# A bank for the first block's fourth product, two row statistics taken at other ticks, and a reordered end, in a one-core encoder-layer kernel

## The chip, the cores and the metric

The kernel runs on one core of a Trainium2 chip. The metric is the device time of one execution in microseconds (us). The kernel before was run three times: 2029.69, 2029.9 and 2030.85 us, median 2029.9 us.

The names of the profile: PE is the matrix engine (TensorE), PEld its weight loads, DVE is VectorE, ACT is ScalarE, POOL is GpSimd, and SP is the engine whose queue starts most of the transfers (SPq). L718 means line 718 of the kernel before.

## The reference

One encoder layer over 512 tokens of width 2048, in float32:

```python
xn   = rms_norm(x, attn_norm_g)
u_val, u_gate, q, k, v = split(xn @ w_in)
y_conv = conformer_conv(u_val, u_gate, ...)     # GLU, depthwise conv of 31, layer norm, silu
y_na   = neighborhood_attention(q, k, v, rpb)   # 16 heads on an 8 x 64 grid of tokens
mixed  = concat(rms_norm(y_conv, conv_out_g), rms_norm(y_na, na_out_g))
x = x + mixed @ w_out
up = depthwise_conv(rms_norm(x, ffn_norm_g) @ w_up, ffn_dw_w, ffn_dw_b)   # width 3
gate, val = split(up)                                                     # 5632 each
x = x + (silu(gate) * val) @ w_down
out = rms_norm(x, final_norm_g)
```

## The kernel before, in words

**Layout.** Activations stand transposed: 128 channels on the partitions, the 512 tokens along the free dimension, in tiles of 128x512 (`t2`, 79 buffers). Each float32 product is made of three matmuls of rounded operands: weights are split into a high and a low part (`parts`, L113, one pass on ACT at L116 and one on DVE at L117), activations likewise, and `mm3` (L124, matmuls at L127 to L129) adds high x high, high x low and low x high in a PSUM bank.

**Order.** The program is written in plain order, and a planner with a cost table for each instruction decides the order on each engine: among the instructions that its model takes as ready, the one written first goes first. Each engine then runs its queue strictly in that order. `pin` keeps an instruction behind the one that was written before it on its engine, and `issue_after` keeps a block's instructions behind a given one. On PE this is used by `tick` (L134): after each unit of 24 matmuls of a projection, it takes one further step of the generators in `steps` (attention, statistics) and `asteps` (the convolution group), whose matmuls so stand behind that unit. Each `yield` in a generator is one unit of delay.

**PSUM.** There are three banks with the tag `mm` for products, one bank `po`, two banks `tr` and one pair `sc`. A product that asks for a tag waits until a bank of this tag is released by its last reader.

**Statistics.** `rsqrt_steps` (L179) turns a sum of squares per token into a row of factors: eight small matmuls with a column of ones add over the partitions (L190), `root` (L172) takes 1/sqrt with one Newton step, the result is laid on two diagonal tiles `dg` (L197 to L201), and one tick later two matmuls with ones (L207) spread it over all partitions, in bank `po`, from which ACT copies it (L211).

`group_a` (L372) is the convolution group: mean (L379), squares (L384 to L386), two idle ticks, the statistic `rln`, then for each of eight tiles the norm, silu and the split into `mah` and `mal` (L393 to L396), `RA_AFTER` = 2 idle ticks, and the statistic `ra`. `out_half(ma, read_a)` (L561, called at L590) is the product with the upper half of `w_out`: sixteen times 24 matmuls, each into an `mm` bank that `read_a` (L580) releases by a DVE product with `ra` (L585). The attention's `values` (L494) also uses the bank `po`, which ACT releases at L507.

**The gated MLP.** The up-projection is done with a Strassen-like scheme of seven products per block f of 128 hidden channels; the first four blocks go through `up_apart` (L793). For f = 0 the products 0 to 2 are written side by side (`first_three`, L811), because the last input tiles come late: seven of the eight inner steps for each, then the eighth for each. The products 0 to 5 take `mm` banks, product 6 takes `po` (`begin`, L795). ACT copies the products 0 and 1 away (L823), the product 2 is added by DVE (L825), ACT copies the product 3 (L826), and the products 4 to 6 are read by DVE (L827, L830, L831).

**The end.** The last four blocks' down-projection is made in two ways. For the tokens 0 to 383, sixteen products `pd` of 128x384 are added to `x2` by DVE (L946), squared by ACT and summed into `acc3` (L947). For the tokens 384 to 511 the result is made token-major in four banks, g = 0 to 3 (L970 to L984): four transposes of `x2` and twelve matmuls each (L973, L977 to L979), a square with a sum on ACT (L981) and a product with the gain on DVE (L984). The banks 0 and 1 are the two halves of one `sc` tile, the banks 2 and 3 are `tr` banks. Between these matmuls, `spread` (L956) takes the steps of the statistic `rstd3` of the first 384 tokens: the column sums after (g, k) = (0, 1), the spreading matmuls of L207 after (1, 0). Then eight pairs of channel tiles are finished (`finish`, L925) and sent out, 128x384 each: in five pairs DVE multiplies straight from the PSUM bank (L935) and each half goes out by a transfer of its own (L937), in three pairs (1, 4, 7) ACT has multiplied by the gain before (L932) and POOL multiplies (L933) by a copy `rb` of the factors in SBUF that ACT makes at L966, with one transfer for the pair (L939). The last 128 tokens are scaled after the root over all four sums (L986 to L997) and leave in four transfers (L998).

Of the kernel before, what the change touches and what calls it, by code (L numbers as in the profile page):

```python
# [10 lines left out]
F32 = mybir.dt.float32  # L11
F32R = mybir.dt.float32r
AF = mybir.ActivationFunctionType
ALU = mybir.AluOpType
AX = mybir.AxisListType

P = 128
D = 2048
S = 512
# [9 lines left out]
EPS = 1e-6  # L29
# [13 lines left out]
CH = 4  # L43
# [8 lines left out]
ORDER = "aavaav" + "aq" * 4 + "qqqq"  # L52
NORM_AT = 4
NG = GW // 8
RA_AFTER = 2

PCOLS = [("g1", KD), ("dww", NC_ * CK), ("dwb", NC_), ("lng", NC_), ("lnb", NC_), ("cog", NC_),
         ("nag", NC_), ("g2", KD), ("fww", 2 * NF * 3), ("fwb", 2 * NF), ("g3", KD)]
# [9 lines left out]
def layer(ctx: ExitStack, tc: tile.TileContext, xT, xG, w_in, w_v, w_out, w_up, w_down, par, tab, g3, out, last_out):  # L68
    nc = tc.nc
# [6 lines left out]
    psa = ctx.enter_context(tc.tile_pool(name="psa", bufs=1, space=bass.MemoryType.PSUM))  # L76
# [9 lines left out]
    def t2(name, dt=F32):  # L86
        return tp.tile([P, S], dt, tag="t2k", name=name)

    def t4(shape, name):

        return wpool.tile(shape, F32, tag="raw", name=name, bufs=NR)

    pin = tc.keep_in_program_order
# [5 lines left out]
    def pc(name, i):  # L99
        o = POFF[name] + i  # L100
        return prm[:, o:o + 1]
# [4 lines left out]
    ident = consts.tile([P, P], F32, name="ident")  # L106
# [41 lines left out]
    def weights():  # L148
        at = weights.at
        weights.at += 1  # L150
        while len(made) < min(at + 1 + AHEAD, len(plan)):
            made.append(plan[len(made)]())
        return made[at]
# [3 lines left out]
    def split(src, g, name):  # L157

        h, l = t2(name + "h", F32R), t2(name + "l", F32R)
        nc.scalar.activation(h, src, AF.Copy, scale=g)  # L160
        nc.vector.scalar_tensor_tensor(l, src, g, h.bitcast(F32), op0=ALU.mult, op1=ALU.subtract)
        return h, l

    def sum_sq(acc, src, first, to=slice(0, S)):
        if first:
            nc.scalar.activation(acc, src, AF.Square)
        else:
            q = t2("sq")[:, to]
            nc.scalar.activation(q, src, AF.Square)
            nc.vector.tensor_add(acc, acc, q)  # L170

    def root(r, y, v):  # L172
        nc.scalar.activation(r, v, AF.Sqrt)
        nc.vector.reciprocal(r, r)
        nc.vector.scalar_tensor_tensor(y, r, -0.5, r, op0=ALU.mult, op1=ALU.mult)
        nc.vector.tensor_mul(y, y, v)
        nc.vector.scalar_tensor_tensor(y, y, 1.5, r, op0=ALU.add, op1=ALU.mult)
# [56 lines left out]
    ps = psa.tile([P, 2, S], F32, tag="sc", name="idle")  # L234
# [22 lines left out]
    for step in ORDER:  # L257
# [5 lines left out]
        i = next(a_ if step == "a" else q_)  # L263
# [108 lines left out]
    def group_a():  # L372
        acc = t2("acc")
        nc.vector.tensor_add(acc, ys[0], ys[1])
        for i in range(2, NC_):
            nc.vector.tensor_add(acc, acc, ys[i])
        yield
        ps = psa.tile([P, S], F32, tag="po", name="st")
        nc.tensor.matmul(ps, ones, acc, start=True, stop=True)  # L379
        mu = t2("mu")  # L380
        nc.vector.tensor_scalar(mu, ps, 1.0 / CONV, None, op0=ALU.mult)
        acc = t2("acc")
        for i in range(NC_):
            nc.vector.tensor_sub(ys[i], ys[i], mu)  # L384
            sum_sq(acc, ys[i], i == 0)
            if i == NC_ // 2 - 1:  # L386
                yield
        yield
        yield
        r = yield from rsqrt_steps(acc, CONV, "rln")  # L390
        acc = t2("acc")
        for i in range(NC_):
            nc.vector.tensor_mul(ys[i], ys[i], r)  # L393
            nc.scalar.activation(ys[i], ys[i], AF.Silu, scale=pc("lng", i), bias=pc("lnb", i))
            ma.append(split(ys[i], pc("cog", i), "ma"))
            sum_sq(acc, ys[i], i == 0)  # L396
            if i % 2:
                yield
        for _ in range(RA_AFTER):
            yield  # L400
        ra.append((yield from rsqrt_steps(acc, CONV, "ra")))


# [151 lines left out]
    x2 = []  # L555
# [237 lines left out]
    def up_apart(f, between):  # L793

        def begin(c):  # L795
            return weights(), (psa.tile([P, S], F32, tag="po", name="pu") if c == 6 else
                               psm.tile([P, S], F32, tag="mm", name="pu"))[:, :H]

        def part(c, w, ps, ks):
            for k in ks:  # L800
                m = comb[c][k]
                i = mm3(ps, w, k, m[:, :H], m[:, H:], k == 0, k == U - 1)
            return i

        def product(c):
            w, ps = begin(c)
            tick(part(c, w, ps, range(U)))
            between(c)
            return ps

        def first_three():  # L811
            got = [begin(c) for c in range(3)]
            for c in range(3):
                tick(part(c, *got[c], range(U - 1)))
            for c in range(3):
                part(c, *got[c], range(U - 1, U))
            return [ps for _, ps in got]

        vv, v, uu, g = (t2(n).rearrange("p (i t) -> p i t", i=2) for n in ("vv", "vl", "uu", "g"))
        both = lambda x: x.unsqueeze(1).broadcast_to([P, 2, H])  # L820
        early = iter(first_three() if f == 0 else map(product, range(3)))
        for i in range(2):
            nc.scalar.activation(vv[:, i], next(early), AF.Copy)  # L823
        u, u2 = uu[:, 0], uu[:, 1]
        add(v, vv, both(next(early)))  # L825
        nc.scalar.activation(u, product(3), AF.Copy)  # L826
        add(u2, u, product(4))  # L827
        add(v, v, both(u2))
        add(vv[:, 1], vv[:, 1], u2)
        add(g[:, 0], u, product(5))  # L830
        add(g[:, 1], vv[:, 1], product(6))  # L831
        return tuple(t.rearrange("p i t -> p (i t)") for t in (g, v))
# [62 lines left out]
    x2, ws = [], []  # L895
# [27 lines left out]
    fm, tm = slice(0, LT), slice(LT, S)  # L923

    def finish(pair, r, apart=False, split=False):  # L925

        o = t4([P, 2, LT], "fin")
        for i in range(2):
            d = 2 * pair + i
            x, g = x2[d][:, fm], pc("g3", d)  # L930
            if apart:
                nc.scalar.activation(x, x, AF.Copy, scale=g)  # L932
                nc.gpsimd.tensor_mul(o[:, i], x, r)  # L933
            else:
                nc.vector.scalar_tensor_tensor(o[:, i], x, g, r, op0=ALU.mult, op1=ALU.mult)  # L935
            if split:
                nc.sync.dma_start(out[pair][:, i], o[:, i])  # L937
        if not split:
            nc.sync.dma_start(out[pair], o)  # L939

    acc = t2("acc3")
    for d in range(KD):
        ps = psm.tile([P, S], F32, tag="mm", name="pd")[:, fm]
# [7 lines left out]
    stats, rb, xg = rsqrt_steps(acc, D, "rstd3", to=fm, keep=False), [], []  # L951
    sums, v, r, y = (sm.tile([P, CH], F32, tag="rs" + c, name="rs" + c) for c in "lvry")
    v, r, y = (t[:, :1] for t in (v, r, y))
    pairs = list(range(KD // 2))

    def spread(g, k):  # L956
        if (g, k) == (0, 1):
            next(stats)
        elif (g, k) == (1, 0):
            try:  # L960
                next(stats)
            except StopIteration as e:
                rb.append(e.value)
            finish(pairs.pop(0), rb[0], split=True)
            rb.append(t2("rb")[:, fm])
            nc.scalar.activation(rb[1], rb[0], AF.Copy)  # L966
        elif rb and pairs:
            at = pairs.pop(0)
            finish(at, rb[at % 3 == 1], at % 3 == 1, at % 3 != 1)

    for g, ps in enumerate(banks):
        for i in range(CH):
            nc.tensor.matmul(ps[:, i * P:(i + 1) * P], x2[g * CH + i][:, tm], ident, start=i == 0, stop=False,  # L973
                             is_transpose=True)
        for k in range(n):
            (hh, hl), (dh, dl) = hs[k], ws[g * CH + k]
            nc.tensor.matmul(ps, hh[:, tm], dh, start=False, stop=False)  # L977
            nc.tensor.matmul(ps, hl[:, tm], dh, start=False, stop=False)
            nc.tensor.matmul(ps, hh[:, tm], dl, start=False, stop=k == n - 1)  # L979
            spread(g, k)  # L980
        nc.scalar.activation(t2("sq"), ps, AF.Square, accum_out=sums[:, g:g + 1])  # L981
        xg.append(t2("xg"))
        if g < CH - 1:
            nc.vector.tensor_mul(xg[g], ps, gains[g])  # L984
        if g == CH - 2:
            nc.vector.tensor_reduce(v, sums[:, :CH - 1], axis=AX.X, op=ALU.add)  # L986
            nc.vector.tensor_scalar(v, v, 1.0 / D, EPS, op0=ALU.mult, op1=ALU.add)
    assert not pairs
    nc.vector.scalar_tensor_tensor(v, sums[:, CH - 1:], 1.0 / D, v, op0=ALU.mult, op1=ALU.add)
    root(r, y, v)  # L990
    for g in range(CH):
        if g == CH - 1:
            nc.vector.scalar_tensor_tensor(xg[g], banks[g], y, gains[g], op0=ALU.mult, op1=ALU.mult)
# [79 lines left out]
```

## Time and profile before

| | |
|---|---|
| time, median of three runs | 2029.9 us |
| the profiled execution | 2030.16 us, of which the profile's span is 2028.4 us |
| PE busy | 2015.4 us (99% of the span) |
| DVE, ACT, POOL busy | 1675.5, 1050.9, 159.5 us |
| granted PE clock, mean | 0.998 |
| output | 4.19 MB in 17 transfers |

How to read it: an engine's busy time is the sum of the time in which at least one of its instructions ran. In rows of the timeline the columns are the start in us from the start of the span, the duration in us, the engine, the line, the operation, what is written and read, the shapes and the count; in brackets stands the time for which the engine had been idle before, and what ended this. Matmuls overlap: each row of a 128x512 matmul says 0.39 us, but the next one starts 0.227 us later, and this distance of the starts is what a matmul costs.

### The profile page before, as it was taken

The numbers are of one execution on the slowest core, as the hardware profiler recorded it, in microseconds if no ns is written. First come the engines' busy times: TensorE is split into PE (matmuls) and PEld (weight loads), VectorE is DVE, ScalarE is ACT, GpSimd is POOL, SyncE is SP. The second block draws the span as 40 slices with busy tenths as digits, with TensorE's granted clock in tenths as the row PEclk, the third lists the DMA queues.
The fourth block names the chain that finished last, engine by engine and source line by source line (L and its number), as shares of the span: only waits on it lengthen the run. The fifth ranks groups of instructions, "written<-read, shape, count | busy, mean of one in ns | idle before, by whom it ended". The sixth has DMA issues, their size and how long they took to land.

```text
span 2028.4 us, 28313 instructions
## 1 busy us (share of the span) xinstructions
PE 2015.4 (99%) x10672; PEld 1726.5 (85%) x10672; DVE 1675.5 (83%) x2298; ACT 1050.9 (52%) x1674; POOL 159.5 (8%) x188
## 2 busy tenths in 40 slices
PE   9999999999999999999999999999999999999998
PEld 7888888888888998888888888888888888888887
DVE  7986888988577898888888888888888888889875
ACT  7323344466346555555555555555555555555563
POOL 0000000000001001111111111111111111110111
PEclk9999999999999999999999999999999999999999
DMA  7232333336347435566565565565565565564583
GB/s 256 83 104 84 114 94 109 109 124 215 108 120 178 120 114 146 123 147 146 125 146 146 128 142 146 128 142 146 121 149 146 125 146 146 127 144 127 144 206 126
DMA packets 97784, 276.41 MB, mean 136 GB/s; under 512 B 10992, under 2 KB 12784, under 8 KB 97648
## 3 DMA queue, kind: packets, MB, share of 16 engines
q1 hardware_dynamic: 72288, 228.45, 36.3%
q0 software_dynamic: 25216, 46.15, 15.5%
q8 instruction: 84, 1.38, 0.3%
q14 instruction: 52, 0.43, 0.1%
q10 hardware_dynamic: 144, 0.01, 0.0%
HBM read 220.04 MB, written 54.53 MB: 135 GB/s over the span
## 4 chain that ended last, share of the span: by engine, by line
PE 96%; DVE 2%; DMA 1%; ACT 0%; issue 0%; SPq 0%; ACTq 0%; DVEq 0%
PE pu L718 25%; PE pu L724 13%; PE pd L129 8%; PE pd L127 8%; PE pd L128 8%; PE pj L127 5%; PE pj L128 5%; PE pj L129 5%; PE po L127 3%; PE po L128 2%; PE po L129 2%; PE pv L313 1%; PE pv L312 1%; PE pv L314 1%; PE pu L127 1%; PE pu L129 1%
## 5 line engine op out<-in xcount | busy, mean ns | idle before, releaser
L116 ACT ACTIVATE whi<-raw 128x1024 fp32r<-128x1024 f32 x364 | 384.4, 1058 | 503.8 <-PE pj L128 136.6
L117 DVE TENSOR_TENSOR wlo<-raw,whi 128x1024 fp32r<-128x1024 f32 x364 | 444.4, 1221 | 214.0 <-ACT whi L116 205.2
L718 PE MATMUL pu<-xc,whi 128*128 128x512 f32 x2240 | 552.9, 391 | 0.0
L718 PEld LDWEIGHTS pu<-xc,whi 128*128 128x128 f32 x2240 | 413.0, 188 | 79.1
L724 PEld LDWEIGHTS pu<-xc,wlo 128*128 128x128 f32 x2240 | 292.3, 191 | 13.9
L724 PE MATMUL pu<-xc,wlo 128*128 128x256 f32 x2240 | 296.6, 283 | 0.0
L129 PE MATMUL pd<-hh,wlo 128*128 128x512 f32 x640 | 250.1, 391 | 0.0
L127 PE MATMUL pd<-hh,whi 128*128 128x512 f32 x640 | 249.6, 390 | 0.0
L128 PE MATMUL pd<-hl,whi 128*128 128x512 f32 x640 | 249.3, 390 | 0.0
L871 POOL DMA_DIRECT2D x2d<-pdc x160 | 139.4, 873 | 1162.4 <-ACT pdc L870 837.4
L128 PE MATMUL pj<-xl,whi 128*128 128x512 f32 x512 | 200.2, 391 | 0.1
L129 PE MATMUL pj<-xh,wlo 128*128 128x512 f32 x512 | 200.0, 391 | 0.0
L127 PE MATMUL pj<-xh,whi 128*128 128x512 f32 x512 | 198.9, 393 | 0.0
L750 ACT ACTIVATE pl<-pu 128x256 f32<-128x256 f32 x280 | 104.6, 382 | 143.5 <-PE pu L718 136.4
L116 ACT ACTIVATE whi<-ws 128x1024 fp32r<-128x1024 f32 x132 | 139.8, 1059 | 75.2 <-PE pu L718 58.2
L366 DVE SCALAR_TENSOR_TENSOR y<-ch,prm,y 128x500 f32<-128x500 f32 (+14 forms) x240 | 173.3, 740 | 4.3
L117 DVE TENSOR_TENSOR wlo<-ws,whi 128x1024 fp32r<-128x1024 f32 x132 | 161.1, 1220 | 13.9 <-ACT whi L116 13.6
L129 PEld LDWEIGHTS pd<-hh,wlo 128*128 128x128 f32 x640 | 120.1, 188 | 28.5 <-DVE wlo L117 3.3
L128 PEld LDWEIGHTS pd<-hl,whi 128*128 128x128 f32 x640 | 120.2, 188 | 24.9 <-DVE hl L856 0.3
L127 PEld LDWEIGHTS pd<-hh,whi 128*128 128x128 f32 x640 | 120.4, 188 | 22.6
L870 ACT ACTIVATE pdc<-pd 128x512 f32<-128x512 f32 x160 | 93.8, 588 | 79.3 <-PE pd L129 65.9
L127 PEld LDWEIGHTS pj<-xh,whi 128*128 128x128 f32 x512 | 96.3, 188 | 20.7 <-ACT xh L249 0.2
(204 smaller groups left out, 2886.4 us busy)
## 6 DMA issues: line engine op xcount, KB each, us to landing
raw<-in_w_up SPq DMA_DIRECT2D x176, 512.0 KB, 3.7
raw<-in_w_down SPq DMA_DIRECT2D x88, 512.0 KB, 4.0
x2d<-pdc POOLq DMA_DIRECT2D x160, 256.0 KB, 4.8
raw<-in_w_in SPq DMA_DIRECT2D x60, 512.0 KB, 3.8
raw<-in_w_out SPq DMA_DIRECT2D x32, 512.0 KB, 3.8
raw<-in_w_v SPq DMA_DIRECT2D x16, 512.0 KB, 4.1
tab<-in_tab SPq DMA_DIRECT2D x32, 256.0 KB, 5.0
x<-in_xG SPq DMA_DIRECT2D x16, 256.0 KB, 5.4
```

The lines of the kernel that those rows point to most:

```text
L116: i = nc.scalar.activation(hi[:, :n], raw[:, :n], AF.Copy)
L117: j = nc.vector.tensor_sub(lo[:, :n], raw[:, :n], hi[:, :n].bitcast(F32))
L127: nc.tensor.matmul(ps, hi[:, a], mh, start=start, stop=False)
L128: nc.tensor.matmul(ps, hi[:, a], ml, start=False, stop=False)
L129: return nc.tensor.matmul(ps, lo[:, a], mh, start=False, stop=stop)
L312: nc.tensor.matmul(ps, xh, wh[:, f], start=kk == 0, stop=False)
L366: nc.vector.scalar_tensor_tensor(y[:, a:b], h[:, a + j - PAD:b + j - PAD], prm[:, o + j:o + j + 1], y[:, a:b], op0=ALU.mult, op1=ALU.add)
L718: i = nc.tensor.matmul(ps, w[0][:, k * P:(k + 1) * P], comb[c][k], start=k == 0, stop=stop and k == ks[-1])
L724: i = nc.tensor.matmul(ps[:, H:], w[1][:, k * P:(k + 1) * P], comb[c][k][:, :H], start=False, stop=stop and k == U - 1)
L750: nc.scalar.activation(to, ps, AF.Copy)
L870: nc.scalar.activation(t, ps, AF.Copy)
L871: nc.gpsimd.dma_start(xd[d], t, accum_op=ALU.add)
```

## The change

- In `group_a` there are three idle ticks instead of two ahead of `rln`, and none instead of two ahead of `ra`. Counted from the generator's first step, `rln` is asked for at step 6 instead of 5, and `ra` at step 11 instead of 12.
- In `up_apart`, the product 3 of f = 0 takes the bank `po`, and its product 6 takes an `mm` bank. The other blocks keep `po` for product 6.
- At the end, the spreading matmuls of `rstd3` are written after (2, 2) instead of (1, 0). The first matmul of (2, 3) is pinned behind them, and the first transpose of g = 3 is pinned behind the matmuls of (2, 3). The copy `rb` is written ahead of all `finish` work, and two pairs are written at each following step instead of one.
- The reduction over the first three sums is written ahead of the product with the gain of g = 2.
- The last root takes its Newton step with other operations: v is multiplied by -0.5, then two fused operations, so that four DVE instructions stand behind the square root as before.

```diff
@@ group_a
-        yield
-        yield
+        for _ in range(3):
+            yield
         r = yield from rsqrt_steps(acc, CONV, "rln")
...
-        for _ in range(RA_AFTER):
-            yield
         ra.append((yield from rsqrt_steps(acc, CONV, "ra")))
@@ up_apart
-            return weights(), (psa.tile([P, S], F32, tag="po", name="pu") if c == 6 else
+            return weights(), (psa.tile([P, S], F32, tag="po", name="pu") if c == (6 if f else 3) else
                                psm.tile([P, S], F32, tag="mm", name="pu"))[:, :H]
@@ spread
-        elif (g, k) == (1, 0):
+        elif (g, k) == (2, 2):
             try:
                 next(stats)
             except StopIteration as e:
                 rb.append(e.value)
-            finish(pairs.pop(0), rb[0], split=True)
             rb.append(t2("rb")[:, fm])
             nc.scalar.activation(rb[1], rb[0], AF.Copy)
-        elif rb and pairs:
-            at = pairs.pop(0)
+        for at in pairs[:2 if rb else 0]:
+            pairs.remove(at)
             finish(at, rb[at % 3 == 1], at % 3 == 1, at % 3 != 1)
@@ for g, ps in enumerate(banks)
+            if g == CH - 1 and i == 0:
+                pin(m)
...
+            if (g, k) == (2, 3):
+                pin(i)
...
         nc.scalar.activation(t2("sq"), ps, AF.Square, accum_out=sums[:, g:g + 1])
+        if g == CH - 2:
+            nc.vector.tensor_reduce(v, sums[:, :CH - 1], axis=AX.X, op=ALU.add)
+            nc.vector.tensor_scalar(v, v, 1.0 / D, EPS, op0=ALU.mult, op1=ALU.add)
         xg.append(t2("xg"))
         if g < CH - 1:
             nc.vector.tensor_mul(xg[g], ps, gains[g])
-        if g == CH - 2:
-            nc.vector.tensor_reduce(v, sums[:, :CH - 1], axis=AX.X, op=ALU.add)
-            nc.vector.tensor_scalar(v, v, 1.0 / D, EPS, op0=ALU.mult, op1=ALU.add)
...
-    root(r, y, v)
+    nc.scalar.activation(r, v, AF.Sqrt)
+    nc.vector.tensor_scalar(v, v, -0.5, None, op0=ALU.mult)
+    nc.vector.reciprocal(r, r)
+    nc.vector.scalar_tensor_tensor(y, r, v, r, op0=ALU.mult, op1=ALU.mult)
+    nc.vector.scalar_tensor_tensor(y, y, 1.5, r, op0=ALU.add, op1=ALU.mult)
```

More of the change, by code (lines that the diff above doesn't have):

```diff
@@ L54 @@
 NG = GW // 8
-RA_AFTER = 2
 PCOLS = [("g1", KD), ("dww", NC_ * CK), ("dwb", NC_), ("lng", NC_), ("lnb", NC_), ("cog", NC_),
@@ L972, in layer @@
         for i in range(CH):
-            nc.tensor.matmul(ps[:, i * P:(i + 1) * P], x2[g * CH + i][:, tm], ident, start=i == 0, stop=False,
-                             is_transpose=True)
+            m = nc.tensor.matmul(ps[:, i * P:(i + 1) * P], x2[g * CH + i][:, tm], ident, start=i == 0, stop=False,
+                                 is_transpose=True)
+            if g == CH - 1 and i == 0:
+                pin(m)
         for k in range(n):
             (hh, hl), (dh, dl) = hs[k], ws[g * CH + k]
-            nc.tensor.matmul(ps, hh[:, tm], dh, start=False, stop=False)
+            i = nc.tensor.matmul(ps, hh[:, tm], dh, start=False, stop=False)
+            if (g, k) == (2, 3):
+                pin(i)
             nc.tensor.matmul(ps, hl[:, tm], dh, start=False, stop=False)
```

## Prediction

> **What bounds the kernel now.** I read the page's first part, then the waits of PE, then the timeline around each wait, and last the timeline and the transfer rates of the end. The page says that PE hardly ever stands still:
>
> ```profile
> span 2028.4 us, 28313 instructions
> PE 2015.4 (99%) x10672; PEld 1726.5 (85%) x10672; DVE 1675.5 (83%) x2298; ACT 1050.9 (52%) x1674; POOL 159.5 (8%) x188
> ```
>
> So two things only can be won here: the few gaps in PE's stream, and the end, where PE is done and something else is late. PE's waits inside the stream, and the matmuls on both sides of each:
>
> ```profile
> PE pu L127 <- ACT vv L823: 1.5, 1, 1.5
> PE st L190 <- DVE acc L170: 0.3, 1, 0.3
> PE po L127 <- DVE oa L585: 0.3, 1, 0.3
> ...
> 431.38 0.39 PE L129 MATMUL pj<-xh,wlo 128*128 128x512 f32 x1
> 432.07 1.05 PE L190 MATMUL st<-ones,acc 128*128 128x1 f32 x8 [0.31 <-DVE acc L170]
> 500.57 0.39 PE L129 MATMUL po<-mah,wlo 128*128 128x512 f32 x1
> 501.22 0.50 PE L127 MATMUL po<-mah,whi 128*128 128x512 f32 x1 [0.26 <-DVE oa L585]
> 678.80 0.28 PE L129 MATMUL pu<-xc,wlo 128*128 128x256 f32 x1
> 680.61 0.39 PE L127 MATMUL pu<-xc,whi 128*128 128x256 f32 x1 [1.53 <-ACT vv L823]
> ```
>
> A gap's price is the distance of the two starts less the usual distance (0.23 us for 512 columns, 0.12 for 256): 0.46 us at 432, 0.42 at 501, 1.69 at 681. As PE is the bound before and behind, each of them moves all that follows. The end is read below.
>
> **Part 1, the bank of product 3: 1.69 us less.** The first three products of f = 0 hold all three `mm` banks to their end, so product 3 waits until ACT has copied product 0. ACT gets there late, because two weight splits stand ahead in its queue:
>
> ```profile
> 670.26 1.06 ACT L116 ACTIVATE whi<-raw 128x1024 fp32r<-128x1024 f32 x1 [1.69 <-PE po L128]
> 671.35 1.23 DVE L117 TENSOR_TENSOR wlo<-raw,whi 128x1024 fp32r<-128x1024 f32 x1 [0.18 <-ACT whi L116]
> ...
> 678.28 1.06 ACT L116 ACTIVATE whi<-ws 128x1024 fp32r<-128x1024 f32 x1
> 679.24 1.04 ACT L116 ACTIVATE whi<-raw 128x1024 fp32r<-128x1024 f32 x1
> 680.19 0.64 ACT L823 ACTIVATE vv<-pu 128x256 f32<-128x256 f32 x2
> ...
> L211 ACT ACTIVATE rna<-st x1: 582/582/582, 567.4 to 567.4; 128x512 f32<-128x512 f32 x1
> ```
>
> In `po` nothing is left at that time; its last user was the attention group's statistic `rna`, copied away at 567.4, over 100 us earlier. What is late next for product 3? Its own weights: the last split of an A11 tile that lies before it is the pair at 670.26 and 671.35, done at 672.6. Its last input tile is the one that the eighth steps of products 0 to 2 need too. So it can follow at 678.92. Product 4 then starts 24 x 0.12 = 2.9 us later, at 681.8; its weights come from the split at 678.28 and the DVE pass behind it (about 680.6), and its bank is product 0's, free at about 680.5. Product 6 of f = 0 gets product 2's bank, long free. One debt is made: f = 1 now finds only the banks of products 4, 5 and 6, and its second product needs one that L830 or L831 releases:
>
> ```profile
> 691.47 1.23 DVE L117 TENSOR_TENSOR wlo<-raw,whi 128x1024 fp32r<-128x1024 f32 x1 [1.13 <-ACT whi L116]
> 695.40 0.41 DVE L830 TENSOR_TENSOR g<-uu,pu 128x256 f32<-128x256 f32 x1
> ...
> 696.73 0.28 PE L127 MATMUL pu<-xc,whi 128*128 128x256 f32 x1
> ```
>
> By the count of matmuls (24 each) that second product starts in the last row, at 696.7, so 695.0 after the change, while L830 ends at 695.8 now. If DVE didn't move, 0.8 us of the 1.69 would come back. But the queue up to L830 hangs on the row at 691.47, which waits for a weight split that waits for PE; it moves with PE, to a release at 694.1. I take the whole 1.69 us; bounds 0.9 and 1.69.
>
> **Part 2, the two statistics: 0.3 us less.** `rln` is asked for one tick later. At 432 only the last sum was missing by some tenths of a us, and a tick is at least 24 x 0.227 = 5.4 us, so this gap of 0.46 us goes. The chain behind `rln` moves by one tick, about 6 us with the attention's matmuls in it. `ra` is asked for at step 11, but its sum isn't there then:
>
> ```profile
> 475.36 0.68 DVE L170 TENSOR_TENSOR acc<-acc,sq 128x512 f32<-128x512 f32 x1
> 479.32 0.95 PE L190 MATMUL st<-ones,acc 128*128 128x1 f32 x8
> 483.28 1.14 DVE L201 SCALAR_TENSOR_TENSOR dg<-ident,rsy,dg 128x128 fp32r<-128x128 f32 x4
> 485.79 0.66 PE L501 MATMUL po<-pt,vg 128*64 128x128 f32 x8
> 497.83 0.58 ACT L507 ACTIVATE ao<-po 128x512 f32<-128x512 f32 x1
> 499.18 0.62 PE L207 MATMUL st<-dg,ones 128*128 128x512 f32 x2
> ```
>
> The last sum now ends at 476.0; 6 us later it is 482, inside the first block of `out_half(ma)`, whose last tile `mal` (one instruction ahead of that sum) is needed only by its eighth step, near 485. The column sums L190 then stand near 482, and may stall PE there by what the planner misjudges: nothing, or up to the 0.46 us of the like place at 432. I take 0.15. From L190 to the end of `dg` it is 484.42 - 479.32 = 5.1 us, so `dg` is ready near 487, behind the attention's `values` at 485.8, which take the only bank `po` and hold it until ACT's copy at 498.4. Then L207 comes as late as now, and the gap at 501 stays. If the sum is 1.5 us earlier, L207 comes first, and 0.42 us more is won. I take nothing for it: 0.46 - 0.15 = 0.3; bounds 0 and 0.88.
>
> **Part 3, the end: 1.25 us less.** PE is done at 2019.33 (1.33 us of the stretch from 2018 in the rows below), yet the transfers go on to 2026.87:
>
> ```profile
> 2010.42 0.88 DVE L201 SCALAR_TENSOR_TENSOR dg<-ident,rsy,dg 128x128 fp32r<-128x128 f32 x3
> 2011.53 0.34 PE L207 MATMUL st<-dg,ones 128*128 128x384 f32 x1
> 2012.40 0.34 PE L207 MATMUL st<-dg,ones 128*128 128x384 f32 x1
> 2012.77 1.14 DVE L935 SCALAR_TENSOR_TENSOR fin<-x,prm,st 128x384 f32<-128x384 f32 x2 [0.87 <-PE st L207]
> 2013.94 0.49 ACT L966 ACTIVATE rb<-st 128x384 f32<-128x384 f32 x1 [3.83 <-DVE fin L935]
> 2014.47 2.71 DVE L935 SCALAR_TENSOR_TENSOR fin<-x,prm,st 128x384 f32<-128x384 f32 x5 [0.56 <-ACT rb L966]
> 2014.52 5.88 POOL L933 TENSOR_TENSOR fin<-x,rb 128x384 f32<-128x384 f32 x6 [39.61 <-ACT rb L966]
> 2016.54 0.33 SPq L939 DMA_DIRECT2D out_T<-fin  x1
> 2021.63 0.44 SPq L939 DMA_DIRECT2D out_T<-fin  x1
> 2022.18 2.79 SPq L998 DMA_DIRECT2D out_N<-xg  x4
> ...
> 2014.00:2015.00 1.00, 1.00 (x6) 0.80 (x5) 0.53 (x2) 0.43 (x1) 0.48 (x1) 1.00 0.73 261
> 2018.00:2026.00 8.00, 1.33 (x6) 0.75 (x4) 4.25 (x13) 2.23 (x5) 2.40 (x3) 0.72 1.02 379
> 2026.00:2028.40 2.40, 0.00 (x0) 0.00 (x0) 0.00 (x0) 0.00 (x0) 0.00 (x0) 0.50 0.36 136
> ```
>
> From 2018 to 2026 the transfer engines are full (share 1.02) at 379 GB/s, and the last stretch is 0.36 x 2.4 = 0.87 us of it. The output, not the root, sets the end. It starts at 2014.27 (0.73 of that microsecond) but is not full until about 2018, since POOL's pairs start at 2014.5 and SP, which keeps its order, waits for the first of them until 2016.54. All 4.19 MB at 379 GB/s take 11.07 us.
>
> After the change the two L207 stand together behind (2, 2). In the trace PE runs the banks in the order 0, 2, 1, 3: bank 1 shares a tile with bank 0 and waits for its product on DVE. So (2, 2) belongs to the second group run, and its last matmul now starts at about 2011.53, in place of the first L207. Both `dg` are done at 2011.30, so the pin that holds (2, 3), and behind it bank 3, waits for nothing on PE. The factors are there some 0.47 us sooner than at 2012.77. ACT copies first (0.49 us), DVE waits for this as it does now at 2014.47, and starts at about 2012.8 as today, but without the 0.56 us hole; POOL starts at 2012.9 instead of 2014.5.
>
> Best case: transfers run full from 2014.27 and end at 2014.27 + 11.07 = 2025.3, 1.5 us sooner. Poor case: SP's order puts each POOL pair (1.94 us for two) ahead of DVE halves that are ready, which leaves some 0.5 us of holes: 1.0 us. I take 1.25. DVE's ten `fin` (0.53 apart), two products and the small sums fill it from 2012.8 to about 2020, just when the last square is done, so the root isn't later. The sums ahead of the product save 0.3 us at most on the root, and the new Newton step keeps four instructions: both are hidden by the transfers.
>
> [...] Eight full microseconds at 379 GB/s decide against it; I give it 0.02, inside the case "all won".
>
> **Sum.** 1.69 + 0.3 + 1.25 = 3.2 us. The profiled execution took 2030.16 (the span and 1.8 us around it) and would take 2026.9; the median of the three runs is 0.26 lower: 2026.7 us, 0.16% faster. A measurement of this kernel can tell about 0.2% (4.1 us) from no change, so this counts as within.
>
> **Rivals.** [...]
>
> - *All of it is won*: the gap at 501 too, no new stall, transfers full at once: 1.69 + 0.88 + 1.5 = 4.1 us, 2025.8. It needs the sum for `ra` by 480.5, against a count of 482.
> - *The factors come later, not sooner*: if the planner runs bank 1 ahead of (2, 2), L207 moves behind twelve more matmuls and four transposes, 3.1 us, and full transfers begin near 2017.3, ending at 2028.4: 1.5 us lost, in all 2029.4. For it speaks that bank 1 is written first; against, that its transposes come behind L207 in the trace.
> - *Product 3 finds another wait* and keeps its gap: 2028.4. Against: weights at 672.6.
> - *Slower*: the sum for `ra` ends only after PE has reached `values` at 485.8. Then L190 itself waits for `po` until 498.4, `dg` is done at 503.6, the gap at 501 starts the fourth block 2.0 us after that (as 501.22 follows 499.18), at 505.6: 5 us more, 2031.7. It decides at a slip of 10 us of the sum, where I count 6. [...]
> - *The change does nothing there*: 2029.9.
>
> **Chances.** Forecast 0.68 (2025.9 to 2027.9); all won 0.10; factors later 0.08; product 3 waits 0.06; slower 0.05; nothing 0.03. The range 2025.3 to 2029.5 takes in all but the last two. Faster by over 0.2%: 0.13 (half of "all won" and the forecast's lucky edge); slower by over 0.2%: 0.04; within: 0.83.
>
> **What would show it.** Right: no row "pu L127 <- ACT vv L823" and no gap near 432 in PE's waits; L207 twice without a matmul between; rb ahead of the first `fin`; a full DMA share from 2015 on. Wrong: a wait for `po` near 490 to 505, a gap near 695, or L207 behind 2014.

## The result: 9.3 us slower, and the profile after

The changed kernel took 2039.72 us (median of six runs, 2038.21 to 2042.89), the kernel before beside it 2030.38 us (six runs, 2029.69 to 2030.85): ratio 1.0049, 95% interval 1.0036 to 1.0062. The forecast was 2026.7 and its range ended at 2029.5. The profiled execution of after (2042.89 us, span 2041.1) is the longest of the six; a weight that lands late near 678 is in it (DVE idles 2.42 us for it), and the 12.7 us between the two traces are 3.4 more than the medians differ by.

The waits of PE in the changed kernel (most lines of its file stand one to four lower than before, the last ones level or some higher):

```profile
PE po L126 <- DVE oa L582: 3.4, 1, 3.4
PE st L206 <- DVE dg L196: 2.1, 1, 2.1
...
PE st L206 <- DVE dg L200: 1.6, 1, 1.6
```

The two rows that the change was to remove are gone: no wait for `acc` at 432, none for `vv` at 681. The one for `oa`, which was to stay, has grown from 0.3 to 3.4 us. All three long waits name DVE, and two of them name a statistic (`rstd2`, the `dg` of L196 and L200) which the change doesn't touch.

**Near 503.** The timeline of the changed kernel:

```profile
477.03 0.68 DVE L169 TENSOR_TENSOR acc<-acc,sq 128x512 f32<-128x512 f32 x1
...
484.66 0.39 PE L206 MATMUL st<-dg,ones 128*128 128x512 f32 x1
...
486.24 0.60 ACT L210 ACTIVATE ra<-st 128x512 f32<-128x512 f32 x1 [0.55 <-PE st L206]
...
499.52 0.39 PE L128 MATMUL po<-mah,wlo 128*128 128x512 f32 x1
...
500.69 0.58 ACT L504 ACTIVATE ao<-po 128x512 f32<-128x512 f32 x1
501.30 0.63 ACT L168 ACTIVATE sq<-ao 128x512 f32<-128x512 f32 x1
501.96 0.69 DVE L169 TENSOR_TENSOR accna<-accna,sq 128x512 f32<-128x512 f32 x1
502.57 1.28 DVE L582 TENSOR_TENSOR oa<-po,ra 128x512 f32<-128x512 f32 x2
...
503.31 0.50 PE L126 MATMUL po<-mah,whi 128*128 128x512 f32 x1 [3.40 <-DVE oa L582]
...
505.21 0.63 PE L126 MATMUL po<-mah,whi 128*128 128x512 f32 x1
...
505.63 0.63 PE L127 MATMUL po<-mal,whi 128*128 128x512 f32 x1
```

The last sum for `ra` is there at 477.71, the first spreading matmul follows at 484.66, and `ra` lies in SBUF at 486.84, 13.6 us sooner than before; the first product's bank is full by then. Yet DVE reads it at 502.57, behind the attention's copy `ao`, its square and its sum `accna`. PE loses 3.56 us, and from 504.35 on eight matmuls start 0.425 us apart instead of 0.227. The windows (the third figure from the end of a row is the granted clock) show for how long it is 0.50, here and around the next gap:

```profile
504.31:507.72 3.41, 3.41 (x9) 2.67 (x8) 2.03 (x4) 0.00 (x0) 0.00 (x0) 0.50 0.23 91
507.72:511.13 3.41, 3.41 (x19) 2.84 (x18) 0.00 (x0) 0.67 (x1) 0.00 (x0) 1.00 0.00 0
...
702.28:709.11 6.83, 5.99 (x27) 5.88 (x28) 6.83 (x14) 2.42 (x5) 0.00 (x0) 0.50 0.02 6
```

At a granted clock of 0.50, eight matmuls cost 0.2 us more each here (1.6 us), and 25 of half the width 0.093 us more each behind 703.7 (2.3 us).

**Near 701.** The same timeline where `rstd2` is made:

```profile
693.23 0.15 DVE L191 TENSOR_SCALAR rsv<-st 128x4 f32<-128x4 f32 x1
...
694.24 1.22 DVE L116 TENSOR_TENSOR wlo<-ws,whi 128x1024 fp32r<-128x1024 f32 x1
695.37 0.17 DVE L173 RECIPROCAL rsr<-rsr 128x4 f32<-128x4 f32 x1
695.46 1.19 DVE L116 TENSOR_TENSOR wlo<-raw,whi 128x1024 fp32r<-128x1024 f32 x1
696.57 0.16 DVE L174 SCALAR_TENSOR_TENSOR rsy<-rsr 128x4 f32<-128x4 f32 x1
696.64 1.22 DVE L670 TENSOR_TENSOR ws<-ws,raw 128x1024 f32<-128x1024 f32 x1
...
701.03 0.47 PE L206 MATMUL st<-dg,ones 128*128 128x512 f32 x1 [2.10 <-DVE dg L196]
...
701.93 1.14 DVE L200 SCALAR_TENSOR_TENSOR dg<-ident,rsy,dg 128x128 fp32r<-128x128 f32 x4
...
703.12 0.80 PE L206 MATMUL st<-dg,ones 128*128 128x512 f32 x1 [1.63 <-DVE dg L200]
```

Between steps of 0.16 us stand passes over weights of 1.2 us. There are six of them from the first step (693.23) to the last `dg` (703.07); before there were three. PE loses 2.26, 1.87 and 0.37 us at these two matmuls and the one behind them.

**The end**, in the timeline and then in a window (its last two figures are the busy share of the transfer engines and GB/s):

```profile
2016.94 0.80 PE L189 MATMUL st<-ones,acc 128*128 128x1 f32 x6
...
2021.10 0.51 PE L206 MATMUL st<-dg,ones 128*128 128x384 f32 x2
...
2025.55 0.60 ACT L981 ACTIVATE sq<-pt 128x512 f32<-128x512 f32 x1 [6.06 <-PE pt L979]
...
2026.14 0.48 ACT L962 ACTIVATE rb<-st 128x384 f32<-128x384 f32 x1
2026.27 0.69 DVE L987 TENSOR_TENSOR xg<-pt,g3b 128x512 f32<-128x512 f32 x1 [5.00 <-ACT sq L981]
```

```profile
2028.00:2029.00 1.00, 0.72 (x4) 0.26 (x2) 1.00 (x4) 0.24 (x1) 1.00 (x2) 1.00 0.64 227
```

The spreading matmuls stand side by side, as written. But the copy `rb`, whose input is there at 2021.6, runs at 2026.14: ACT first takes the square of bank 1, for which it waits until PE has filled that bank. DVE waits in the same way with bank 1's product (L987). PE ends at 2028.72, the span 12.4 us later; before it was 9.1.

Summed up: 4.3 us net near 503 (3.56 + 1.6, less the gaps of 0.42 and 0.47 that are gone), 5.7 near 681 to 710 (6.8, and 0.8 us of waits near 682, less 1.69 and 0.2), 3.3 at the end, 0.5 at the start (a wait for `xh`). That is 13.8 us, 1.1 more than the traces differ by. By the starts of the same matmul in both traces the changed kernel is 3.7 us behind at 508 and 9.2 at 709, so the 1.1 us lie ahead of 508: PE had won time at the start before it lost the 0.5 there, and the rest are small differences.

### The profile page after: what moved, and what is told of

Its sections match the earlier page's. It is cut to its first block, busy times and chain, and to the rows that moved or that the text cites. A ratio compares the mean times of both kernels' runs of the same rounds, so it can differ in the third digit from the quotient of the medians.

```text
span 2041.1 us, 28320 instructions
## 1 busy us (share of the span) xinstructions
PE 2019.1 (99%) x10672; PEld 1729.7 (85%) x10672; DVE 1676.1 (82%) x2298; ACT 1051.9 (52%) x1675; POOL 159.6 (8%) x188
## 4 chain that ended last, share of the span: by engine, by line
PE 94%; DMA 2%; DVE 2%; issue 1%; ACT 0%; POOL 0%; SPq 0%; ACTq 0%; DVEq 0%; POOLq 0%
PE pu L715 25%; PE pu L721 13%; PE pd L128 8%; PE pd L126 8%; PE pd L127 8%; PE pj L126 6%; PE pj L127 6%; PE pj L128 6%; PE po L126 2%; PE po L127 2%; PE po L128 2%; PE pv L311 1%; PE pv L313 1%; PE pv L312 1%; PE pu L126 1%
```

## The experiments

Theory A: three separate losses, one of each part, and each the order of one in-order queue. Rival B: one loss upstream that spreads. The times (11 runs each, and 33 of the kernel before beside them):

| run | us | before | ratio (95%) |
|---|---|---|---|
| stats_only | 2035.05 | 2030.18 | 1.0023 (1.0014 to 1.0031) |
| bank_only | 2032.97 | 2030.18 | 1.0013 (1.0004 to 1.0022) |
| end_only | 2033.23 | 2030.18 | 1.0014 (1.0005 to 1.0023) |
| end_late | 2029.08 | 2030.18 | 0.9992 (0.9984 to 1.0001) |
| stats_first | 2029.22 | 2030.16 | 0.9995 (0.9986 to 1.0004) |
| ra1_rln | 2033.45 | 2030.16 | 1.0016 (1.0007 to 1.0025) |
| bank_pool | 2030.20 | 2030.16 | 0.9999 (0.9990 to 1.0008) |
| end_late_poolq | 2029.42 | 2030.16 | 0.9995 (0.9986 to 1.0003) |
| end_tile | 2028.96 | 2030.10 | 0.9993 (0.9984 to 1.0002) |
| best | 2029.74 | 2030.10 | 0.9996 (0.9987 to 1.0005) |
| best_bank | 2027.91 | 2030.10 | 0.9988 (0.9979 to 0.9997) |
| first_only | 2030.23 | 2030.10 | 1.0002 (0.9994 to 1.0011) |

### Each part alone

The diff of each is the part of the change's diff that its name says.

> The kernel before with only the two statistics moved (three idle ticks ahead of rln, none ahead of ra). Theory A, three separate losses, each from the order in one engine's queue: the 3.4 us wait of PE for DVE's first product with ra appears near 503 as in the changed kernel, with some slow matmuls behind it, while the gap near 681 (1.7 us) and the end stay as before; about 4 us slower, 2034.4. Theory B, one loss upstream that spreads: the moved statistics alone make the later steps late too, the waits near 701 and the later end appear here as well; about 9 us slower, 2039.7. My forecast on record would be 0.3 us faster, 2030.1.

> The kernel before with only the bank of product 3 of f = 0 changed (and product 6 in its place). Theory A: the gap near 681 goes (1.7 us less), and in its place PE waits twice for DVE's diagonal tiles of rstd2 near 698 (4.5 us more): about 2.8 us slower, 2033.2. Theory B: the waits near 701 came from the stages ahead, which arrived late; alone the bank is the gain that I forecast, 1.7 us, 2028.7.

> The kernel before with only the end changed. Theory A: ACT has the square of the second bank ahead of the copy rb in its queue, so the copy and all output wait some 4.5 us for a bank that PE has not filled yet; the stretch behind PE's end grows from 9.1 to about 12.4 us: 3.3 us slower, 2033.7. Theory B: the end is late only because what stands ahead of it is; alone it gives the 1.25 us that I forecast, 2029.1.

Measured: 4.9, 2.8 and 3.05 us slower, each with its whole interval above 1. Rival B falls: each part loses alone, at the place where the whole loses. Together that is 10.7 us, inside the interval of the whole (7.3 to 12.6). In the profile of stats_only PE waits 3.4 us for `oa` (and 2.3 instead of 1.5 for `vv`, as a weight lands late at 678), in that of bank_only 1.4 and 1.6 us for `dg`, and in that of end_only the copy runs at 2015.79, 2.6 us ahead of PE's end.

### The end: what holds the copy

end_late writes the square and the product of bank 1 behind the copy, in (2, 2); `close(g)` holds the lines that stood at the end of the loop over the banks:

```diff
             nc.scalar.activation(rb[1], rb[0], AF.Copy)
+            close(1)
...
+        if g == 1:
+            continue
+        close(g)
```

> As the run with only the end changed, but the square and the gain product of the second bank are written behind the copy rb, so that ACT has the copy ahead of that square. Theory A: the copy runs about half a microsecond behind the spreading matmuls, transfers are full some 1.5 us sooner than before, and the time is about 1.2 us under the kernel before, 2029.2. Rival C: not ACT's queue but POOL's pairs and the order of the transfers hold the end; then this run stays near the run with only the end changed, 2033.7.

end_tile leaves every instruction where the change wrote it, and lets GpSimd write zeros into the copy's tile ahead of the banks:

```diff
+    copy_ = t2("rb")[:, fm]
+    nc.gpsimd.memset(copy_, 0.0)
...
-            rb.append(t2("rb")[:, fm])
+            rb.append(copy_)
```

> The end as in the change, with every instruction written where the change has it; only, the tile for the copy rb gets a first write (zeros, by GpSimd, which idles) ahead of the four banks, so that its place in the pool isn't asked for between those of bank 1 and bank 2. Theory A (a pool gives its places in the written order of the first writes, so the copy stood behind the square and the product of bank 1, which waited for PE): the copy comes ahead of that square, and the time is that of the run where the square was written later, 2029.1. Rival H (the written order of the two ACT instructions, or the shared bank, decides): ACT's queue is as in the change and the time 2033.2.

Measured: 2029.08 and 2028.96 us, 4.2 and 4.3 us less than end_only; Rivals C and H fall. Against the kernel before that is 1.10 and 1.14 us less. Both intervals just reach 1, so the times alone don't settle this gain, but the traces show it: behind PE's end the span runs on for 7.9 us in both, where it was 9.1 before. In end_tile the copy and bank 1's square are written as in the change, and only the first write of the copy's tile moved; that alone turns the two around on ACT. So here the pool gives its places in the written order of the first writes: `rb` had to wait for its place until bank 1's `sq` and `xg` had theirs, and these were planned for when PE would have filled the bank. The end of end_tile in the timeline and by windows:

```profile
2011.99 0.51 PE L207 MATMUL st<-dg,ones 128*128 128x384 f32 x2
...
2012.59 0.49 ACT L968 ACTIVATE rb<-st 128x384 f32<-128x384 f32 x1 [2.21 <-issue]
...
2013.11 3.76 DVE L935 SCALAR_TENSOR_TENSOR fin<-x,prm,st 128x384 f32<-128x384 f32 x7 [0.95 <-ACT rb L968]
```

```profile
2014.00:2015.00 1.00, 1.00 (x6) 0.82 (x5) 1.00 (x3) 0.00 (x0) 1.00 (x2) 1.00 0.40 146
2015.00:2016.00 1.00, 1.00 (x6) 0.81 (x5) 1.00 (x3) 0.00 (x0) 1.00 (x2) 1.00 0.69 247
2016.00:2024.00 8.00, 3.61 (x18) 2.64 (x16) 5.76 (x16) 3.49 (x9) 3.06 (x4) 0.98 1.02 378
```

This is the end that the prediction described, down to the holes that POOL's first pair leaves in SP's order until 2016. end_late_poolq sends POOL's three pairs through POOL's own queue:

> The end with the copy rb ahead of the second bank's square, and the three pairs that POOL multiplies leave through POOL's own queue instead of SP's. In the run without this, transfers were full only 2.4 us after the first one, since SP waits for POOL's first pair. Theory A: they are full at once, some 0.7 us sooner, 2028.4. Rival G: POOL's queue needs as long to issue its transfers as SP lost by waiting, no difference to 2029.1.

Its windows:

```profile
2014.00:2015.00 1.00, 1.00 (x6) 0.81 (x5) 1.00 (x3) 0.00 (x0) 0.72 (x1) 1.00 0.84 301
...
2018.00:2024.00 6.00, 1.23 (x6) 0.67 (x4) 4.25 (x12) 2.22 (x5) 3.13 (x4) 0.88 0.94 347
```

The holes at the beginning are mostly filled, but from 2018 to 2024 the transfers run at 347 GB/s (378 from 2016 to 2024 in end_tile), and behind PE's end the span runs on for 8.4 us instead of 7.9. The time, 2029.42 us, doesn't differ from that of end_late by more than the noise. A miss for Theory A. The time is as Rival G says, but whether for its reason isn't shown: each issue holds POOL for 0.6 us, and the rate is lower too. What lowers the rate wasn't tried.

### The statistics

stats_first has both statistics moved, and reads a product ahead of the tick:

```diff
-            tick(i)
-            read(d, ps)
+            if read is read_a:
+                read(d, ps)
+            tick(i)
+            if read is not read_a:
+                read(d, ps)
```

> Both statistics moved as in the change, and beside that the first products of out_half are read (DVE's product with ra) ahead of the tick, so that their tiles are handed out ahead of those of the attention step of the same tick. Theory A (tiles of one pool are handed out in written order, so the read stands behind the attention's copy and sum in DVE's queue): the wait at 503 shrinks from 3.4 us to well under 1, its slow matmuls behind it go, and the time is within 1 us of the kernel before, about 2030. Rival D: ra itself or PE's own order holds the bank, the wait stays, 2035.0.

ra1_rln moves `rln` alone, with `RA_AFTER = 1`:

> Only rln is asked for one tick later; with one idle tick ahead of ra, ra is asked for at step 12 as before. Theory A with the loss caused by the earlier ra: the gap near 432 (0.47 us) goes and nothing else moves, 2029.7. Rival E: the later rln alone makes the attention's softmax late and the read with it, the wait of some 3 us near 503 is there, 2034.

first_only has the read ahead of the tick and nothing moved:

> The kernel before with only the read ahead of the tick, the statistics not moved. ra is the last thing there that the read waits for, so the gap at 501 (0.42 us) and that at 432 (0.47 us) should stay: 2030.2. If the read's place alone is the gain of the run with both: 2029.3.

stats_first takes 2029.22 us, 5.8 less than stats_only; Rival D falls. It is 0.9 us under the kernel before, again with an interval that reaches 1. DVE now reads the first product ahead of the attention's sum, and PE waits 0.16 us (timeline of stats_first):

```profile
499.43 0.68 DVE L588 TENSOR_TENSOR oa<-po,ra 128x512 f32<-128x512 f32 x1
...
500.17 0.50 PE L127 MATMUL po<-mah,whi 128*128 128x512 f32 x1 [0.16 <-DVE oa L588]
...
502.65 0.68 DVE L170 TENSOR_TENSOR accna<-accna,sq 128x512 f32<-128x512 f32 x1
```

The edit moves the read's place in the written order and the order in which its tile is asked for together, so that it is the tile and not the written order itself is taken over from end_tile, and not shown here. Nor does the read follow at once: `ra` is there at 486.93, and what holds the read until 499.43 stays open.

The read alone does nothing (first_only), as expected. ra1_rln was a miss: I had put the loss down to the earlier `ra`, but the later `rln` alone costs 3.3 us. In its profile PE waits 1.4 us for `ao` ahead of L207 and 1.4 us for `oa`. ACT's queue there (timeline of ra1_rln):

```profile
500.11 1.06 ACT L116 ACTIVATE whi<-raw 128x1024 fp32r<-128x1024 f32 x1 [1.70 <-PE po L128]
501.07 0.58 ACT L507 ACTIVATE ao<-po 128x512 f32<-128x512 f32 x1
```

`ao` is copied about as late as in the changed kernel (500.69; before 497.83). In both, ACT has it behind a weight split that waits for PE, where in the kernel before it followed the softmax directly, ahead of that split. In ra1_rln `ra` still stands behind `values`, so PE waits for `ao` to release `po`, and then for `oa`. So the later `rln` makes the attention late, and in the changed kernel the earlier `ra` can't help since the read stands behind the attention. Why the planner puts the split ahead of `ao` wasn't tried.

### The bank

bank_pool has the bank changed, and the three steps on DVE behind the reciprocal of `rstd2` become four on GpSimd:

```diff
+        nc.gpsimd.tensor_mul(y, r, r)
+        nc.gpsimd.tensor_mul(y, y, v)
+        nc.gpsimd.tensor_scalar(y, y, -0.5, 1.5, op0=ALU.mult, op1=ALU.add)
+        nc.gpsimd.tensor_mul(y, y, r)
```

> The bank of product 3 changed, and beside that the four small steps behind the reciprocal of rstd2 run on GpSimd in place of DVE, so that no weight pass can stand between them. Theory A (PE's two waits near 696 come from the 1.2 us weight passes that stand between the small steps in DVE's queue): the waits shrink from 3.4 us to under 1, and the gain of the bank is left, about 2028.8. Rival F: PE arrives there too early for any order of DVE, and what was won at 681 is given back: 2030.2 to 2033.

Its waits of PE:

```profile
PE pd L128 <- DVE hl L864: 0.7, 1, 0.7
...
PE st L215 <- DVE dg L205: 0.3, 1, 0.3
```

The waits for `dg` shrink from 1.4 and 1.6 us to 0.3, the granted clock is 1.00 from 680 to 764, and the 2.8 us of loss are gone. So the passes between the small steps were the loss. But the gain of 1.7 us isn't left, and the time, 2030.20 us, is that of Rival F: a wait for DVE's low halves comes up at 764, which takes back 1.1 us with the slips behind it, and 0.6 us stay near 693. From 740 to 764 DVE was busy 23.78 of 24 us before the change, and is 24.00 now (windows of before, then of bank_pool):

```profile
740.00:764.00 24.00, 24.00 (x175) 22.80 (x174) 23.78 (x32) 14.13 (x20) 0.00 (x0) 1.00 0.40 126
```

```profile
740.00:764.00 24.00, 23.32 (x167) 21.47 (x165) 24.00 (x32) 13.74 (x19) 0.00 (x0) 1.00 0.39 121
```

Where DVE has nothing to spare, taking a wait from PE doesn't shorten this stage. That this holds for any order of DVE's queue is argued, not shown.

### The parts together

best is stats_first with end_late; best_bank adds bank_pool.

> Both repaired parts together, without the bank: the statistics with the read ahead of the tick, and the end with the second bank's square behind the copy. If the two gains add: 2030.2 - 0.9 - 1.1 = 2028.2. If the gain in the middle is given back before the end, as with the bank: 2029.1.

> All three parts of the change, each repaired: as the run with the two repaired parts, and the bank of product 3 with the small steps of rstd2 on GpSimd. If DVE is what gives back the 1.7 us of the bank (at 764, where PE waited for DVE's low halves): no more than 0.3 us from the run without the bank, 2028.2. If that wait was an accident of one order: 1 to 1.5 us under it, 2027.

best_bank took 2027.91 us, 0.12% under the kernel before (0.03 to 0.21%), the only version whose interval stays under 1, and about the sum of the two gains (0.9 + 1.1). best was to be 2028.2 and gave 2029.74, a miss: five of its eleven runs took 2027.6 to 2028.3 us, the others 2029.7 to 2031.5. In its profiled execution (2031.50 us) a weight lands late (DVE idles 2.5 us for it until 674.3), PE waits near 677 and 681, and the granted clock is 0.50 behind that, from 682.08 to 685.49. That the other long runs of best have the same cause is likely, but only this one has a trace. A late load there is in the profiled executions of after (DVE idles 2.4 us for it, 0.8 in the kernel before), stats_only, end_late and best_bank too, and why it comes in some and not in others stays open. In best_bank DVE idles 2.7 us for it, but product 3 has its bank, so PE waits only 0.4 us, and the granted clock is 1.00 from 692 to 701. So the bank may pay where a weight is late; no run tries this by itself. best_bank is 1.8 us under best's median, but within the span of best's five short runs.

## Why the prediction was wrong, step by step

- **Part 1, the gap at 681** was read rightly: it goes, all 1.69 us. The debt was named with the wrong creditor. I checked the bank that f = 1 needs, near 695, and let "the queue up to L830" move with PE. The step that failed: I took DVE's queue as fixed, shifted as a whole. With product 4 earlier the planner put other passes between the small steps of `rstd2`, and PE, 1.7 us ahead, waited 1.4 and 1.6 us for `dg`. That costs more than was won, and behind it the granted clock is 0.50 from 696.08 to 702.90 (a like stretch cost 2.3 us in the changed kernel): alone, 2.8 us slower.
- **Part 2, the gap at 432** goes as forecast, and the column sums for `ra` stall nothing (0.15 us had been set aside). The first step that failed: the last sum was to end "6 us later", at 482. `rln`'s own column sums did move by 6.1 us (432.07 to 438.19), but the last sum ended at 477.71, only 1.7 us later. So "L207 comes as late as now" failed too: it came 14.5 us sooner (at 484.66), ahead of `values`. That meets the condition of the case "all of it is won" (the sum by 480.5), and yet the gap at 501 grew eightfold. That is the second step that failed: I took it that DVE reads the bank as soon as `ra` is there, and left the attention where it was. The attention's copy came 2.9 us later, and the read stood behind it.
- **The slower rival** had the right place and price (5 us at the fourth block; 3.6 came, and 1.6 of clock) and the wrong mechanism: not the bank `po`, but DVE's queue (in ra1_rln `po` does hold PE, for 1.4 us). Its condition, a slip of the sum by 10 us, was never near, so its chance of 0.05 said nothing about this loss.
- **Part 3.** The matmuls side by side: right; the second stands 4.3 us behind the first column sum (2016.94 to 2021.27), where it stood 4.8 us behind it (2007.57 to 2012.40). "ACT copies first" failed: it is written first among the end's work on pairs, but its tile wants a place behind bank 1's. That turned a gain of 1.25 us into a loss of 3.05. With the tile's place asked for earlier, the stretch behind PE's end is 1.1 us shorter than before: the terms behind that step were about right. The rival in which the factors come later looked for the delay on PE, where there was none. No run shows the end, given 0.02, whose transfers run faster than 379 GB/s: at full share they moved 378 in the changed kernel (2030 to 2038) and in end_tile.
- **The clock.** I gave it no place in the forecast. In the changed kernel a wait of 3.40 us ends at 503.31, and the granted clock is 0.50 from 504.31 to 507.72; waits of 2.10 and 1.63 us end at 701.03 and 703.12, and it is 0.50 from 702.28 to 709.11. That is 1.6 and 2.3 us of the loss.
- The three losses have one root: I costed the removed waits and kept the order of the queues from the trace of before, though a planner makes that order anew.

## What to carry to other kernels

Where a planner writes the queues, an edit that makes something ready sooner or later can change the order on engines that it doesn't name. So ask for each engine what now stands ahead of the instruction that you hope to speed up, and in which written order the tiles it writes get their places. On an engine that is nearly always busy, look first at small dependent steps with long passes between them; here they were what came late. And short waits of PE that lie close together can cost in clock as well, as here: 2.3 us in the changed kernel, beside waits of 2.1 and 1.6 us.

## What the runs showed of the hardware

**The granted clock behind short waits.** In the profiled execution of bank_only waits of 1.4 and 1.6 us were followed by a granted clock of 0.50, while it stayed 1.00 beside two waits of 1.4 us in ra1_rln. And of two waits of 2.3 us, the one in best was followed by 0.50 and the one in stats_only was not. Where it was 0.50 within PE's stream in the changed kernel, it was so for 3.41 us (from 504.31) and for 6.83, twice that (from 702.28), and the two starts lie 197.97 us apart, 58 times 3.413. So the windows below are of that length. The first figure is their length and the second PE's busy time. First bank_only and ra1_rln, each around its two short waits (the second row of bank_only is twice as long):

```profile
692.66:696.08 3.42, 1.62 (x11) 1.14 (x9) 3.42 (x5) 1.06 (x1) 0.00 (x0) 1.00 0.64 206
696.08:702.90 6.82, 5.62 (x25) 5.52 (x26) 6.82 (x14) 2.38 (x4) 0.00 (x0) 0.50 0.02 8
```

```profile
498.25:501.66 3.41, 2.05 (x10) 1.35 (x8) 1.78 (x4) 1.70 (x4) 0.00 (x0) 1.00 1.06 390
501.66:505.07 3.41, 1.95 (x7) 1.34 (x8) 3.35 (x6) 1.23 (x2) 0.00 (x0) 1.00 0.72 278
```

Then best and stats_only, each around its wait of 2.3 us:

```profile
678.67:682.08 3.41, 1.08 (x10) 0.88 (x9) 3.06 (x6) 3.03 (x6) 0.00 (x0) 1.00 0.34 100
682.08:685.49 3.41, 3.41 (x19) 3.41 (x18) 2.96 (x4) 0.00 (x0) 0.00 (x0) 0.50 0.05 17
```

```profile
680.98:684.40 3.42, 2.00 (x15) 1.59 (x13) 2.77 (x8) 3.42 (x9) 0.00 (x0) 1.00 0.70 173
684.40:687.81 3.41, 2.50 (x21) 2.51 (x22) 3.41 (x5) 1.12 (x3) 0.00 (x0) 1.00 0.17 65
```

In bank_only and best PE idled 1.80 and 2.33 us of the first window, and the granted clock of the next was 0.50. In ra1_rln and stats_only the waits are spread over two windows, with 1.36 and 1.46, and 1.42 and 0.91 us idle, and it was 1.00 in both. In the changed kernel 2.41 us idle from 500.90 to 504.31 and 2.88 us from 698.87 to 702.28 were followed by 0.50. It was still 0.50 in the window after one with 0.84 us idle (702.28 to 705.69), and 1.00 again after one without (705.69 to 709.11). In the kernel before PE ends at 2019.33, and the mean from 2021.5 to 2022 is 0.58. An estimate from these numbers: here PE's idle time within such a window counted, not the length of one wait, and so what a wait cost in clock hung on where it fell. In ra1_rln and stats_only the clock doesn't change beside the windows, so where they begin is a part of the estimate; a border isn't shown.

**GpSimd beside a pass of DVE.** In bank_pool the first small step on GpSimd took 1.08 us and ended at 691.01, 0.06 us behind DVE's pass; the next one, of the same kind and size, took 0.20 us:

```profile
689.76 1.19 DVE L117 TENSOR_TENSOR wlo<-raw,whi 128x1024 fp32r<-128x1024 f32 x1
689.93 1.08 POOL L182 TENSOR_TENSOR rsy<-rsr 128x4 f32<-128x4 f32 x1 [16.93 <-DVE rsr L181]
691.09 0.20 POOL L183 TENSOR_TENSOR rsy<-rsy,rsv 128x4 f32<-128x4 f32 x1
```

Whether the pass made the step slow isn't shown: it is also the first on GpSimd after 16.9 us of idle time, and no run takes the two apart.
